# A two-layer encoder on one core: prepared weight sums paused, respaced and extended to the second mixer, and one affine step moved to ScalarE

## The chip, the cores and the metric

The kernel runs on one core of a Trainium2 chip. The core has TensorE (PE in the profile, with PEld for its weight loads), VectorE (DVE), ScalarE (ACT), GpSimd (POOL) and SyncE (SP, which here only issues transfers). The metric is device time in microseconds, the median of several runs; before the change it is 2389.23 us (2387.51 to 2389.99 in three runs). The shape is a batch of 1, a sequence of 256 tokens, a model width of 2048, all in float32.

## What is computed

```python
def reference(x, ...):
    h = x
    for layer in range(2):
        hn = rmsnorm(h, norm_mix_g[layer])
        if layer == 0:
            mix = mlstm_mixer(hn, ...)   # 8 heads, matrix memory, both directions, head norm, gate, @ w_out
        else:
            mix = hgrn_mixer(hn, ...)    # 16 heads, gated linear recurrence, both directions, head norm, gate, @ w_out
        h = h + mix
        h = h + conv_glu(rmsnorm(h, norm_ffn_g[layer]), ...)   # (gelu(conv3(a)) * v) @ w_down, width 5504
    return rmsnorm(h, final_g)

def gate(f):                             # inside hgrn_mixer
    log_f = jnp.logaddexp(log(lb), log1p(-lb) + jax.nn.log_sigmoid(f))   # f -> lb + (1 - lb) * sigmoid(f)
    k = (1.0 - lb) * jax.nn.sigmoid(-f)
```

So there are six stages, one after the other: the first mixer, its output projection, the first feed-forward part, the second mixer, its output projection, the second feed-forward part. Each feed-forward part again has two halves (`FA` = 22 and `FB` = 21 blocks of 128 columns), each an up-projection followed by a down-projection.

## The kernel before

**Products and splits.** Every product with a weight is made from two halves of each operand: a value is copied to the PE's reduced float32 type (`wh`, on ACT, L145), and the rest is the difference (`wl`, on DVE, L146). `split_weights` does this in pieces of 1024 columns, in the order in which the products need them, and PE uses three of the four products of halves. A raw weight tile (`raw`, 2048 columns, 1 MB, three buffers) is loaded by SP and holds two pieces. The halves of a piece have four buffers each (`WB`), in some stages two more.

**Chunks.** `stream` walks through a list of chunks. A chunk of kind `fm` makes a 256-wide projection with features on partitions (L342, L346), a chunk of kind `tm` a 512-wide one with tokens on partitions (L358). A chunk of kind `st` (`squares_by_seven`, L232) makes two 512-wide column blocks of a projection at once: its weights come as units, four blocks B11, B22, B21, B12 of 512 columns each. For the units listed in `SEVEN` and `SEVEN_MIX` it uses seven block products in place of eight. For these it needs differences of the weight blocks and, of the activations, the sums that `token_sums` makes.

**Combines and couples.** The differences of the weight blocks are made in one of two ways. Either `combine` (L204) makes them in place, just ahead of the unit's splits: four differences of 128x512 on DVE. Or they are made ahead, in a stage that has time for them, by `prepare`: SP loads the unit into a pair of tiles (`praw`, two loads of 512 KB), DVE makes four differences (L607), SP stores them to a scratch in HBM (`tscr`, two stores of 512 KB), and the down-projection later loads 768 KB of the unit from the weights, 256 KB from the scratch into the same raw tile, and 768 KB from the scratch into a tile `T`. One unit handled in this way is called a couple here. Couples are counted from 1, within the program or, where it is said, within a stage.

There are two sorts. The couples of a feed-forward half are made during its own up-projection (`ahead` is true: the next couple's load is issued before this couple's differences, with two pairs of tiles). The early couples are made in the mixer ahead of the feed-forward part (`prepare_early`, `ahead` is false): one pair of tiles, so a load has to wait until the store before it has landed. The first mixer makes 12 early couples, the second 15. The pairs of the two output projections (`SEVEN_MIX`, three units each) are combined in place.

**Side work and order.** Everything beside the main stream of products is a generator that is pushed to `side`. `tick` advances a planned time with the matmuls that are emitted (0.65 us for a few, 20.8 us for a `tm` chunk and 10.4 us for an `fm` chunk), and a job goes on when its own `yield` time is over. This sets the order in which instructions are emitted. A scheduler then orders them again, engine by engine, by when it expects their inputs; a few are pinned. `late` issues a transfer on SP and keeps it in program order against the other ones issued so. Each engine then runs its instructions in that order, and an instruction that waits holds all those behind it.

**The heads.** In the first mixer `head` makes the scores S of one head (L798), multiplies the weights W with them (L800, DVE), splits the result into `Wh` and `Wl` (L803, ACT; L804, DVE), then makes four products `pn` (L812), each followed by a denominator `rd` (L815, L816) and the scaled output `y` (L818, L820). `finish` norms, gates (L835) and transposes it (L840) and splits it (L365). Two heads run at a time, and the weights W of a later pair are made beside them (L787). In the second mixer `take` makes q and the gates: sigmoid (L982), the other sigmoid (L983), the affine step lb + (1 - lb) * s (L984, DVE), a product on POOL (L985). `head` then multiplies QK by the gates level by level (L1033, DVE; a gathered copy on ACT at L1012; G2 on POOL), makes `pa` and `pd` on PE (L1020, L1044, L1045), merges them into `AD` (L1055, DVE) and `AT` (L1059, ACT), and makes `py` (L1070). `finish` gates and transposes the result (L1085, L1091).

In `mixed`, which makes an output projection, `token` prepares the activation sums (L639, L542). Its temporaries `f` and the combines' tiles `T` share one tag with two buffers.

Of the kernel before, what the change touches and what calls it, by code (L numbers as in the profile page):

```python
# [8 lines left out]
F32 = mybir.dt.float32  # L9
# [6 lines left out]
P = 128  # L16
# [47 lines left out]
def trunk_kernel(ctx, tc, xT, x_d, fg_d, pp_d, cst_d, w_gate, w_first, w_aq, w_ak, w_av, w_ao, w_aout, w_ao2,  # L64
# [22 lines left out]
    def aux(name):  # L87
        return psa.tile([P, 512], F32, tag="aux", name=name)
# [39 lines left out]
    pin = tc.keep_in_program_order  # L128
    turns = dict(w=0)

# [50 lines left out]
    def temporary(pool_, name):  # L181
        return pool_.tile([P, 1536], F32, tag="avc", bufs=TEMP if pool_.name == "ff" else 2, name=name)

# [404 lines left out]
    def prepare(tiles, todo, first, period, finished, start, ahead):  # L588

        loaded = []  # L590

        def load(i):
            if i < len(todo):
                r = tiles(i)
                for j in range(2):
                    start(r[j], todo[i][0][:, j * 1024:(j + 1) * 1024])
                loaded.append(r)

        yield first
        load(0)  # L600
        for i, (_, dst) in enumerate(todo):
            yield period / 2
            if ahead:
                load(i + 1)
            B11, B22, B21, B12 = (loaded[i][j // 2][:, j % 2 * 512:(j % 2 + 1) * 512] for j in range(4))
            for x, y, out in ((B12, B22, B22), (B12, B11, B12), (B11, B22, B11), (B21, B11, B21)):
                dve.tensor_tensor(out, x, y, ALU.subtract)  # L607
                yield period / 24
            for j in range(2):
                nc.sync.dma_start(dst[:, j * 1024:(j + 1) * 1024], loaded[i][j])  # L610
            if not ahead:
                yield period / 3
                load(i + 1)
        finished.append(True)
# [7 lines left out]

    def mixed(w, w2, x, norm, close):

# [6 lines left out]

        two = pair(w2, KT, 1, x, sums, norm, SEVEN_MIX)

        def token():
# [20 lines left out]
    def mlstm(norm, nxt):  # L655
# [135 lines left out]
        def head(st, j):  # L791
            mp, emn = box["mp"], box["emn"]
            hd = 2 * st["pr"] + j
            q, k, V, W = st["q"][j], st["k"][j], st["V"], st["W"][j]
            S = aux("S")
# [27 lines left out]
            for t in range(2):  # L823
                jk = ev.tile([P, 512], F32, tag="jk", bufs=1, name="jk")
                act.activation(jk[:, 0:T], y[:, t], AF.Square, accum_out=ss[:, t:t + 1])
            st["y"][j] = (y, head_scale(ss, 256))

        def finish(st):
            for j in range(2):
                while st["y"][j] is None:  # L830
                    yield
                y, rs = st["y"][j]
                pz = aux("pz")
                for t in range(2):
                    dve.scalar_tensor_tensor(y[:, t], y[:, t], rs[:, t:t + 1], st["sg"][:, t, j * T:(j + 1) * T],  # L835
                                             ALU.mult, ALU.mult)
                yield
                for t in range(2):
                    for v in range(2):
                        pe.transpose(pz[:, v * T + t * P:v * T + (t + 1) * P], y[:, t, v * P:(v + 1) * P], ident)  # L840
                for v in range(2):
                    i = 2 * (2 * st["pr"] + j) + v
                    YT[i] = slot(i, "ya")
                    split(YT[i], pz[:, v * T:(v + 1) * T], col("a_head_g", i))
                yield

        chunks = []
        for pr in range(AH // 2):
# [36 lines left out]
            def done_first(ps, done_v=done_v):  # L885
# [10 lines left out]
                side.push(start(gs))  # L896
                prepare_early(box["mp"], 0, 45.0, 13.0)

# [34 lines left out]
    def hgrn(norm, nxt):  # L933
# [32 lines left out]
        def take(hd, what, ps):  # L966
# [16 lines left out]
            act.activation(kz, z, AF.Sigmoid, scale=-1.0)  # L983
            dve.tensor_scalar(g, g, oml[:, hd:hd + 1], lb[:, hd:hd + 1], ALU.mult, ALU.add)  # L984
            pool.tensor_tensor(QZ[:, (1 - dr) * T:(2 - dr) * T], st["q"], g, ALU.mult)  # L985
# [147 lines left out]

        return chunks + mixed(w_bout, w_bo2, yx, nxt, stack.close)


    def ffn(layer, norm, nxt):
        stack = ExitStack()
        ending = isinstance(nxt, FinalNorm)
        box = dict(n=2 * (len(SEVEN[0]) + len(SEVEN[1])) * layer)  # L1140
        chunks, pairs = [], []
# [36 lines left out]
        for part, (f0, nf) in enumerate(((0, FA), (FA, FB))):  # L1178
# [13 lines left out]
            def two(src, c0, norm, seven, first=0, todo=todo, finished=finished, GT=GT, SX=SX, nf=nf):  # L1192
                ch = pair(src, nf, c0, lambda k: GT[k], lambda u: SX[u], norm, seven)
                ch.waits = [finished]
                for i, u in enumerate(seven):
                    ch.stored[u] = tscr[box["n"]]
                    (early[layer][0] if i < first else todo).append((src[:, 2048 * u:2048 * (u + 1)], tscr[box["n"]]))
                    box["n"] += 1
                if first:
# [117 lines left out]
def build(nc, ins, out_shape=(2, P, D), **kw):  # L1317
# [3 lines left out]
    mscr = nc.dram_tensor("mscr", (64, T), F32, kind="Internal").ap()  # L1321
    tscr = nc.dram_tensor("tscr", (4 * len(SEVEN[0]) + 4 * len(SEVEN[1]), P, 2048), F32, kind="Internal").ap()
    with tile.TileContext(nc, schedule_with_timeline_sim=True) as tc:
# [17 lines left out]
```

## Time and profile before

| | |
|---|---|
| median of the runs | 2389.23 us |
| the profiled execution | 2391.24 us |
| its span, first to last instruction | 2388.9 us |
| granted TensorE clock, mean | 0.998 |
| ScalarE casts `wh` from raw tiles of 1024 columns (L145), 844 of them, with others of the line | 875.1 us |
| VectorE splits `wl` of the same (L146), 844 | 1031.7 us |
| couples' differences (L607), 240 | 167.2 us |

The time of an execution is a little longer than the span of its instructions. Times in the profile are microseconds from the start of the span, means of one instruction are nanoseconds. In the tables by stage a row holds the stretch, its length, the busy time of PE, PEld, DVE, ACT and POOL with the number of instructions in brackets, the granted TensorE clock, the share of time in which the DMA engines were busy, and GB/s. In a table of waits a row reads: who waited, for whom, how long in total, how often, the longest. In a timeline a row begins with the start and the time taken; at its end, in brackets, stands how long the engine was idle before it and what ended that. In a table of groups the idle time before the instructions stands behind the second bar. In the chain of waits a row is a start, a time and what took it. A row of transfers ends with the size of one and the median time from issue to landing.

### The profile page before, as it was taken

To read this page: it belongs to the slowest core of one execution; us is meant where nothing else is said; L and a number is where in the kernel's file an instruction comes from. 1 tells how busy PE (TensorE), PEld (TensorE's weight loads), DVE (VectorE), ACT (ScalarE), POOL (GpSimd) and SP (SyncE) were. 2 spreads that over 40 slices of the span, in tenths; PEclk is the share of its full clock that TensorE was granted. 3 is DMA by queue.
4 is the path that set the end of the run, shared out by engine and by line. 5 is a ranking of instruction groups with operands and counts; after the bars stand their busy time and mean duration, and the time that the engine had idled before them with its cause. 6 is when DMAs were issued, how large, how long until landed. Compare 5 with 4: busy or idle time off the path is not lost.

```text
span 2388.9 us, 38320 instructions
## 1 busy us (share of the span) xinstructions
PE 2367.0 (99%) x14548; PEld 2019.7 (85%) x14548; DVE 1972.0 (83%) x3060; ACT 1442.5 (60%) x2289; POOL 217.3 (9%) x244
## 2 busy tenths in 40 slices
PE   9999999999999999999999999999999999999998
PEld 8878888888888888888888888887888888888886
DVE  7777787897888888787898888878788788888787
ACT  7655555555665555665666666665555566555565
POOL 0100000000000000000243333220000000000000
PEclk9999999999999999999999999999999999999999
DMA  8778756886698887786766777545788588887695
GB/s 306 266 263 294 279 194 212 300 302 231 227 346 288 324 307 248 279 308 222 246 235 253 248 247 248 207 167 180 254 298 289 194 303 315 287 286 252 207 343 199
DMA packets 119240, 624.31 MB, mean 261 GB/s; under 512 B 13440, under 2 KB 13952, under 8 KB 74256
## 3 DMA queue, kind: packets, MB, share of 16 engines
q1 hardware_dynamic: 117360, 617.86, 73.3%
q0 software_dynamic: 1120, 3.21, 0.7%
q8 instruction: 114, 1.87, 0.3%
q10 hardware_dynamic: 576, 0.79, 0.1%
q14 instruction: 70, 0.57, 0.1%
HBM read 556.73 MB, written 65.08 MB: 260 GB/s over the span
## 4 chain that ended last, share of the span: by engine, by line
PE 85%; DMA 7%; DVE 5%; issue 2%; ACT 1%; POOL 0%; SPq 0%; DVEq 0%; POOLq 0%; ACTq 0%
PE mm L342 32%; PE mm L346 16%; PE mm L358 14%; PE pc L232 13%; PE mm L232 7%; DMA praw<-in_w_d 4%; DVE wl L146 2%; DMA tscr<-praw 1%; DVE praw L607 1%; PE py L1070 1%; PE pd L1020 0%; PE pz L419 0%; PE pa L1020 0%; ACT wh L145 0%; DMA T<-tscr 0%
## 5 line engine op out<-in xcount | busy, mean ns | idle before, releaser
L342 PE MATMUL mm<-xt,wh 128*128 128x512 f32 x3776 | 1313.5, 394 | 0.1
L146 DVE TENSOR_TENSOR wl<-raw,wh 128x1024 fp32r<-128x1024 f32 (+1 forms) x844 | 1031.7, 1228 | 217.0 <-ACT wh L145 213.3
L145 ACT CAST wh<-raw 128x1024 fp32r<-128x1024 f32 (+1 forms) x844 | 875.1, 1042 | 486.4 <-PE mm L342 280.6
L346 PE MATMUL mm<-xt,wl 128*128 128x256 f32 x3776 | 1044.5, 278 | 0.3 <-DVE wl L146 0.3
L342 PEld LDWEIGHTS mm<-xt,wh 128*128 128x128 f32 x3776 | 705.7, 188 | 160.5 <-issue 0.2
L346 PEld LDWEIGHTS mm<-xt,wl 128*128 128x128 f32 x3776 | 709.7, 188 | 6.2 <-DVE wl L146 0.9
L358 PE MATMUL mm<-wh,xt 128*128 128x512 f32 x1024 | 323.6, 394 | 0.2 <-ACT wh L145 0.2
L232 PE MATMUL pc<-wh,g 128*128 128x512 f32 x776 | 260.9, 390 | 0.2 <-ACT wh L145 0.2
L607 DVE TENSOR_TENSOR praw<-praw 128x512 f32<-128x512 f32 x240 | 167.2, 697 | 80.6 <-DMA praw<-in_w_d 63.7
L358 PEld LDWEIGHTS mm<-wh,xt 128*128 128x128 f32 x1024 | 191.4, 188 | 40.1 <-ACT xt L364 0.6
L358 PE MATMUL mm<-wl,xt 128*128 128x512 f32 x512 | 198.6, 392 | 0.0
L232 PEld LDWEIGHTS pc<-wh,g 128*128 128x128 f32 x776 | 145.6, 188 | 30.9 <-ACT wh L145 0.6
L232 PE MATMUL pc<-wl,g 128*128 128x512 f32 x388 | 150.9, 389 | 0.0
L232 PE MATMUL mm<-wh,sx 128*128 128x512 f32 x396 | 140.2, 390 | 0.5 <-ACT wh L145 0.4
L146 DVE TENSOR_TENSOR wl<-T,wh 128x512 fp32r<-128x512 f32 (+1 forms) x132 | 124.0, 953 | 20.1 <-ACT wh L145 19.6
L145 ACT CAST wh<-T 128x512 fp32r<-128x512 f32 (+1 forms) x132 | 109.6, 835 | 38.7 <-PE pc L232 14.1
L566 POOL TENSOR_TENSOR hm<-hm,u 128x512 f32<-128x512 f32 x10 | 14.7, 1467 | 1230.1 <-DVE u L565 637.5
L1033 DVE TENSOR_TENSOR QK<-QK,G 128x256 f32<-128x256 f32 x224 | 110.0, 537 | 8.3 <-ACT kq L1012 8.1
L1012 ACT COPY kq<-QK 128x512 f32<-128x512 f32 x112 | 74.6, 669 | 68.5 <-DVE QK L1033 46.6
L358 PEld LDWEIGHTS mm<-wl,xt 128*128 128x128 f32 x512 | 96.5, 188 | 18.9
L1157 ACT COPY avc<-mm 128x256 f32<-128x256 f32 x172 | 64.1, 373 | 77.3 <-PE mm L346 77.1
L232 PEld LDWEIGHTS mm<-wh,sx 128*128 128x128 f32 x396 | 74.2, 188 | 16.6 <-ACT wh L145 1.3
(237 smaller groups left out, 2240.3 us busy)
## 6 DMA issues: line engine op xcount, KB each, us to landing
raw<-in_w_up SPq DMA_DIRECT2D x172, 1024.0 KB, 5.3
praw<-in_w_d SPq DMA_DIRECT2D x120, 512.0 KB, 7.0
tscr<-praw SPq DMA_DIRECT2D x120, 512.0 KB, 6.4
raw<-in_w_bq SPq DMA_DIRECT2D x48, 1024.0 KB, 5.0
raw<-in_w_d SPq DMA_DIRECT2D x60, 768.0 KB, 6.0
T<-tscr SPq DMA_DIRECT2D x60, 768.0 KB, 7.1
raw<-in_w_ao SPq DMA_DIRECT2D x24, 1024.0 KB, 5.3
raw<-in_w_d SPq DMA_DIRECT2D x24, 1024.0 KB, 6.7
```

What stands on the lines that cost most here:

```text
L145: pin(act.copy(wh[:, :m], r))
L146: pin(dve.tensor_tensor(wl[:, :m], r, wh[:, :m].bitcast(F32), ALU.subtract))
L232: pe.matmul(ps, a, b, start=id(ps) not in begun, stop=stop and i == 2)
L342: pe.matmul(ps[f], wh[:, c:c + P], x, start=k + kk == 0, stop=False)
L346: pe.matmul(ps[f][:, 0:T], wl[:, c:c + P], x[:, 0:T], start=False, stop=k + kk == ch.nk - 1)
L358: pe.matmul(ps[t], x[:, a + t * P:a + (t + 1) * P], w[:, c], start=st and i == 0, stop=sp and i == 2)
L566: pool.tensor_tensor(part(1, 0), part(1, 0), u, ALU.add)
L607: dve.tensor_tensor(out, x, y, ALU.subtract)
L1012: act.copy(m, blocks(QK, h))
L1033: dve.tensor_tensor(two[:, j], two[:, j], by[:, j], ALU.mult)
L1070: pe.matmul(py[:, c], AT[:, s if s == t else 2 + s], V[:, s, j * P:(j + 1) * P], start=(s == 0), stop=(s == 1))
L1157: act.copy(z, p[:, T:2 * T])
```

## The change

- `turns["busy"]` counts the first mixer's heads that are at work: `head` raises it at its start and lowers it at its end, `finish` does so for each of its two heads. An unfinished couple emits no further difference while the count is above 0.
- In `prepare`, the early couples wait a period less 6 us between load and differences (in place of half a period), 0.6 us between differences, and 3 us between the store and the next load (in place of a third of a period). The waiting third of a period now stands in the branch for the couples of a feed-forward half, which had none at this place. The first mixer's early couples start at 40 in place of 45 with a period of 12 in place of 13, the second's have a period of 18 in place of 20.
- The three units of the second output projection become early couples of the second mixer, ahead of the 15 that it makes. The pair waits until all early couples are done.
- Temporaries outside the feed-forward parts get a tag by their name, with two buffers each.
- The affine step of the second mixer's gate goes from DVE to ACT.

```diff
-    turns = dict(w=0)
+    turns = dict(w=0, t=0, busy=0)
...
     def temporary(pool_, name):
-        return pool_.tile([P, 1536], F32, tag="avc", bufs=TEMP if pool_.name == "ff" else 2, name=name)
+        ff = pool_.name == "ff"
+        return pool_.tile([P, 1536], F32, tag="avc" if ff else name, bufs=TEMP if ff else 2, name=name)
...
         for i, (_, dst) in enumerate(todo):
-            yield period / 2
             if ahead:
+                yield period / 2
                 load(i + 1)
+            else:
+                yield period - 6.0
             B11, B22, B21, B12 = (loaded[i][j // 2][:, j % 2 * 512:(j % 2 + 1) * 512] for j in range(4))
             for x, y, out in ((B12, B22, B22), (B12, B11, B12), (B11, B22, B11), (B21, B11, B21)):
+                while turns["busy"]:
+                    yield 0.6
                 dve.tensor_tensor(out, x, y, ALU.subtract)
-                yield period / 24
+                yield period / 24 if ahead else 0.6
             for j in range(2):
                 nc.sync.dma_start(dst[:, j * 1024:(j + 1) * 1024], loaded[i][j])
-            if not ahead:
+            if ahead:
                 yield period / 3
+            else:
+                yield 3.0
                 load(i + 1)
...
+    def store(ch, src, u, todo):
+        ch.stored[u] = tscr[turns["t"]]
+        turns["t"] += 1
+        todo.append((src[:, 2048 * u:2048 * (u + 1)], ch.stored[u]))
...
-    def mixed(w, w2, x, norm, close):
+    def mixed(w, w2, x, norm, close, layer=None):
...
+        if layer is not None:
+            for u in SEVEN_MIX:
+                store(two, w2, u, early[layer][0])
+            two.waits = [early[layer][1]]
...
         def head(st, j):
...
+            turns["busy"] += 1
...
             st["y"][j] = (y, head_scale(ss, 256))
+            turns["busy"] -= 1
...
-                prepare_early(box["mp"], 0, 45.0, 13.0)
+                prepare_early(box["mp"], 0, 40.0, 12.0)
...
-            prepare_early(mp, 1, 30.0, 20.0)
+            prepare_early(mp, 1, 30.0, 18.0)
...
-            dve.tensor_scalar(g, g, oml[:, hd:hd + 1], lb[:, hd:hd + 1], ALU.mult, ALU.add)
+            act.activation(g, g, AF.Identity, bias=lb[:, hd:hd + 1], scale=oml[:, hd:hd + 1])
...
-        return chunks + mixed(w_bout, w_bo2, yx, nxt, stack.close)
+        return chunks + mixed(w_bout, w_bo2, yx, nxt, stack.close, 1)
```

More of the change, by code (lines that the diff above doesn't have):

```diff
@@ L832, in finish @@
                 y, rs = st["y"][j]
+                turns["busy"] += 1
                 pz = aux("pz")
@@ L844, in finish @@
                     split(YT[i], pz[:, v * T:(v + 1) * T], col("a_head_g", i))
+                turns["busy"] -= 1
                 yield
@@ L1139, in ffn @@
         ending = isinstance(nxt, FinalNorm)
-        box = dict(n=2 * (len(SEVEN[0]) + len(SEVEN[1])) * layer)
+        box = {}
         chunks, pairs = [], []
@@ L1195, in two @@
                 for i, u in enumerate(seven):
-                    ch.stored[u] = tscr[box["n"]]
-                    (early[layer][0] if i < first else todo).append((src[:, 2048 * u:2048 * (u + 1)], tscr[box["n"]]))
-                    box["n"] += 1
+                    store(ch, src, u, early[layer][0] if i < first else todo)
                 if first:
@@ L1321, in build @@
     mscr = nc.dram_tensor("mscr", (64, T), F32, kind="Internal").ap()
-    tscr = nc.dram_tensor("tscr", (4 * len(SEVEN[0]) + 4 * len(SEVEN[1]), P, 2048), F32, kind="Internal").ap()
+    tscr = nc.dram_tensor("tscr", (len(SEVEN_MIX) + 4 * len(SEVEN[0]) + 4 * len(SEVEN[1]), P, 2048), F32, kind="Internal").ap()
     with tile.TileContext(nc, schedule_with_timeline_sim=True) as tc:
```

## The prediction

> **What bounds the kernel.** I read the page's busy shares, then busy time by stage, then PE's waits in each stage, then the lines of DVE just ahead of those waits.
>
> ```profile
> span 2388.9 us, 38320 instructions
> PE 2367.0 (99%) x14548; PEld 2019.7 (85%) x14548; DVE 1972.0 (83%) x3060; ACT 1442.5 (60%) x2289; POOL 217.3 (9%) x244
> ...
> 60.00:331.00 271.00, 266.38 (x1352) 223.30 (x1352) 203.12 (x377) 147.20 (x243) 19.24 (x25) 1.00 0.77 268
> 331.00:394.00 63.00, 63.00 (x292) 52.27 (x291) 57.25 (x81) 38.87 (x57) 3.56 (x2) 1.00 0.55 191
> 394.00:1093.00 699.00, 698.68 (x3736) 599.99 (x3735) 585.36 (x839) 413.31 (x596) 16.43 (x9) 1.00 0.80 284
> 1093.00:1613.00 520.00, 517.58 (x4684) 444.64 (x4683) 439.03 (x758) 349.85 (x666) 155.30 (x177) 1.00 0.66 230
> 1613.00:1683.00 70.00, 67.17 (x303) 53.78 (x302) 60.73 (x89) 39.05 (x59) 3.54 (x2) 1.00 0.50 176
> 1683.00:2378.00 695.00, 694.70 (x3717) 596.77 (x3716) 576.23 (x827) 407.11 (x585) 15.49 (x13) 1.00 0.77 272
> ```
>
> The stages are, in order, the first mixer, its output projection, the first feed-forward part, the second mixer, its output projection, the second feed-forward part. In each row the length comes first and PE's busy time second. PE is the bound throughout; what can be won is its idle time: 4.6, 0, 0.3, 2.4, 2.8 and 0.3 us. Idle time of DVE or ACT is worth nothing by itself. PE's waits in the first, fourth and fifth of these stages:
>
> ```profile
> PE pz L840 <- DVE y L835: 1.6, 2, 0.9
> PE pn L812 <- DVE Wl L804: 1.4, 2, 1.1
> PE pn L812 <- DVE y L820: 0.7, 1, 0.7
> PE pn L812 <- ACT Wh L803: 0.6, 1, 0.6
> ...
> PE py L1070 <- ACT AT L1059: 2.1, 1, 2.1
> ...
> PE pc L232 <- ACT wh L145: 1.4, 2, 1.0
> PE pc L232 <- DVE wl L146: 1.0, 1, 1.0
> PE mm L232 <- ACT wh L145: 0.4, 1, 0.4
> ```
>
> In the mixers' heads they have one cause. DVE works in order and stands at a couple's first difference (L607) until its load lands; the head's own DVE work is queued behind it:
>
> ```profile
> 166.43 0.69 DVE L607 TENSOR_TENSOR praw<-praw 128x512 f32<-128x512 f32 x1 [3.71 <-DMA praw<-in_w_d]
> ...
> 295.62 0.69 DVE L607 TENSOR_TENSOR praw<-praw 128x512 f32<-128x512 f32 x1 [3.62 <-DMA praw<-in_w_d]
> ...
> 145.45 0.62 PE L358 MATMUL mm<-wh,xt 128*128 128x512 f32 x2
> ...
> 295.72 0.40 PE L358 MATMUL mm<-wl,xt 128*128 128x512 f32 x1
> 297.24 0.51 PE L812 MATMUL pn<-Vh,Wl 128*128 128x258 f32 x2 [1.13 <-DVE Wl L804]
> ...
> 1259.86 0.69 DVE L607 TENSOR_TENSOR praw<-praw 128x512 f32<-128x512 f32 x1 [3.55 <-DMA praw<-in_w_d]
> ...
> 1262.91 1.16 PE L1070 MATMUL py<-V,AT 128*128 128x128 f32 x8 [2.10 <-ACT AT L1059]
> ```
>
> A late load (3.62) makes the split Wl late, and PE stands for 1.13. A stall costs somewhat more than its idle time, because matmuls overlap: two take 0.62, one 0.40, so they start 0.22 apart, and idle counts only from the end of the last one, 0.18 later. I add 0.2 per stall. The ceiling is then 4.3 + 6 x 0.2 = 5.5 us in the first mixer and 2.8 + 4 x 0.2 = 3.6 us in the second output projection. In the second mixer the stall brought a second loss:
>
> ```profile
> 1260.50:1262.90 2.40, 0.31 (x2) 0.00 (x0) 2.40 (x8) 0.99 (x5) 0.00 (x0) 1.00 0.03 14
> ...
> 1264.25:1267.65 3.40, 3.40 (x10) 2.62 (x9) 3.40 (x7) 2.47 (x5) 0.00 (x0) 0.50 0.73 251
> ```
>
> After a stretch with 0.31 us of PE work in 2.40, the granted clock was 0.50 for 3.40 us, which is 1.7 us of work lost. This event cost 2.1 + 0.2 + 1.7 = 4.0 us. [...] All that can be won is 5.5 + 4.0 + 3.6 + 0.6 = 13.7 us.
>
> **The change part by part.** *The pause.* A couple's differences are no longer emitted between the steps of a first-mixer head. In the built order of the kernel before, those of couples 1, 4, 5, 8, 9 and 12 stand among head operations; in the changed order, where the scheduler still hoists what it thinks ready, those of couples 1, 2, 5 and 9 do. The second halves of the heads and the finishing (L835) are nearly free of them. Couples 5 and 9 now stand between the next head's W and the first rd, where couple 1 stood before; the row of that place is the 0.7 of L820, so 0.9 each. Of 5.5 us I take 5.5 - 1.8 = 3.7 as gained. Bounds: 5.5 if nothing stalls, 0 if the hoisted couples cost what the old ones did.
>
> *The couples' cycle.* This is the part that may cost. These rows give the turn of one pair of buffers, and what DVE waited for it in the first and in the second mixer:
>
> ```profile
> 107.78 7.01 DMA tscr<-praw
> ...
> 114.80 5.93 DMA praw<-in_w_d
> ...
> praw<-in_w_d SPq DMA_DIRECT2D x120, 512.0 KB, 7.0
> tscr<-praw SPq DMA_DIRECT2D x120, 512.0 KB, 6.4
> ...
> T<-tscr SPq DMA_DIRECT2D x60, 768.0 KB, 7.1
> ...
> L607 DVE TENSOR_TENSOR praw<-praw 128x512 f32<-128x512 f32 x48 | 33.0, 687 | 36.9 <-DMA praw<-in_w_d 28.3 <-issue 8.5
> ...
> L607 DVE TENSOR_TENSOR praw<-praw 128x512 f32<-128x512 f32 x60 | 43.8, 730 | 11.2 <-DMA praw<-in_w_d 10.4 <-issue 0.7
> ```
>
> Store, then load, then differences: 6.4 + 7.0 = 13.4 us from a couple's last difference to the next one's first, if the load is issued when the store lands. Early couples used to pause a third of the period before a load (4.3 planned us in the first mixer, 6.7 in the second); now it is 3.0 in both. The second mixer takes 520 us for 416 planned (8 chunks of 20.8, 24 of 10.4), a factor of 1.25: 8.3 us of pause was over 6.4, 3.75 is not. So SP will stand at each load for up to 6.4 - 3.75 = 2.7 us, with the weights' raw loads queued behind it and ACT's casts waiting for those; three raw buffers of two pieces each cover it. The longer lead (12 planned us for 10) does not decide, since the scheduler sets a difference on DVE where it expects the load. What decides is the DVE work between couples. These rows price it:
>
> ```profile
> L146 DVE TENSOR_TENSOR wl<-raw,wh 128x1024 fp32r<-128x1024 f32 x167 | 208.9, 1253 | 39.0 <-ACT wh L145 38.1
> L1033 DVE TENSOR_TENSOR QK<-QK,G 128x256 f32<-128x256 f32 x224 | 110.0, 537 | 8.3 <-ACT kq L1012 8.1
> ...
> L1055 DVE COPY_PREDICATED AD<-cst,pd 128x64 f32<-128x64 int32 x80 | 18.1, 227 | 7.3 <-ACT AD L1053 6.0
> L984 DVE TENSOR_SCALAR G<-G,oml,lb 128x256 f32<-128x256 f32 x32 | 15.9, 498 | 0.5 <-ACT G L982 0.5
> ```
>
> In the second mixer of the kernel before, every gap between couples holds six to ten splits; in the changed order nine of seventeen gaps hold two to five. The gap before the fourth couple holds 4 splits, 8 QK products and 4 AD copies: 4 x 1.25 + 8 x 0.54 + 4 x 0.23 = 10.2 us, 3.2 short of 13.4. Nine such waits are some 29 us of DVE standing, for 11.2 now. In the first mixer twelve couples (36.9 us of such waits) mostly passed PE by: splits run ahead, and only what falls on a head's chain reaches PE. Of the nine, the fourth couple has four AD copies of a nearly finished head close behind it, the place of the 3.55 above; the others stand among QK products or evacuations. I take one event of 4.0 us, as before: no gain, no loss. Bounds: 4.0 gained if none; three events, 8 us lost.
>
> [...]
>
> In the feed-forward parts the swapped branch adds a third of a period to each cycle, so couples spread over the whole part. PE stands there for 0.3 + 0.3 us; I take 0.4 of it, between 0.6 and a loss of 1.
>
> *Second mixer's pair made ahead.* It removes three units' combines from the output projection:
>
> ```profile
> L204 DVE TENSOR_TENSOR T<-raw 128x512 f32<-128x512 f32 x6 | 4.0, 686 | 2.9 <-PE pz L1091 2.9
> ...
> L204 DVE TENSOR_TENSOR T<-raw,T 128x512 f32<-128x512 f32 x3 | 2.0, 686 | 0.0
> L204 DVE TENSOR_TENSOR raw<-raw 128x512 f32<-128x512 f32 x3 | 2.0, 684 | 0.0
> ```
>
> That is 12 differences, 4.0 + 2.0 + 2.0 = 8.0 us of DVE, in a stage in which DVE is busy for 60.7 of 70. PE's stalls there wait for splits, and for casts of differences, that are queued behind them, so I take 3.0 of the 3.6. The first output projection keeps its combines and has no idle at all, so such a stage can run clean; that is the upper bound, 3.6. What comes in: per unit two loads and two stores of 512 KB, and for all three 12 x 0.69 = 8.3 us of DVE, in the second mixer, where DVE is free for 520 - 439 = 81 us; and in the projection a T load (7.1 us) and a quarter of the raw tile from scratch, per unit. They are issued while SP runs ahead; if a T buffer (there are two) came free late, SP would hold raw loads back and nothing would be won: lower bound 0. The couples must be done before the pair starts: 30 + 18 x (17.4 + about 0.8 of rounding to steps) = 358 planned us, of 416.
>
> *The affine step.* 32 operations leave DVE (15.9 us) and go to ACT. The nearest row on ACT, the same function on the same shape with two column operands:
>
> ```profile
> L1162 ACT ACTIVATE avc<-avc,pp 128x256 f32<-128x256 f32 x43 | 25.8, 600 | 26.0 <-DVE avc L1160 25.9
> ```
>
> So 32 x 0.60 = 19.2 us on ACT, which is free for 520 - 350 = 170. The built order has as many table loads as before. Queued behind it are the second sigmoid and the weight casts, each later by 0.6 at most; POOL's product starts about as early. On the path: 0, within half a microsecond either way.
>
> The other edits (own tags for two temporaries, more scratch) issue nothing new. Sum: 3.7 + 0 + 0.4 + 3.0 + 0 = 7.1 us. The profiled execution took 2391.24, 2.0 over the median of the runs, 2389.23: 2391.2 - 7.1 = 2384.1 there, and 2389.2 - 7.1 = 2382.1 as a median.
>
> **Rivals.** First, *the second mixer gives it back*: two events instead of one, 4.0 more, 2386.1. For it: nine short gaps. Against: the other 11.2 - 3.55 = 7.6 us of such waits leave no mark on PE there now. Second, *the heads are no better*: four couples still stand in them, the first mixer gains nothing, 2385.8. Against: the gaps before couples 5 and 9 hold a whole head's DVE work, so their loads should have landed. Third, *slower*: DVE, once late, stays late in the second mixer, because it is 84% busy (439 of 520) and makes up only 1 us in 6. From three more events on (12.0 more), the time is 2382.1 + 12.0 = 2394.1. It decides once a wait of 3 us reaches PE at four of the nine gaps. Fourth, *better*: no event at all, 2378.1.
>
> **How the numbers follow.** Forecast 0.48, rivals 0.17, 0.13, 0.10 and 0.12. A measurement of this kernel tells about 0.2% (4.8 us) from no change, so faster is under 2384.4: forecast and fourth rival, 0.60; same is the first two rivals, 0.30; slower 0.10. The likeliest case spans 2378 to 2384.4; the range, 2376.5 to 2391.5, reaches from just under the ceiling of 13.7 across both same cases and a part of the way to the third rival.
>
> **What would show it.** Right: no PE wait at L840's place and at most two short ones at L812's; no combine rows and no PE wait at L232's in the second output projection; PE's clock at 0.5 at most once in the second mixer; waits of L607's there of 20 to 35 us. Wrong: PE waits of several us at L1044's, L1070's or L1091's in the second mixer, or differences still named ahead of late Wl and y.

## The result, and the profile after

The changed kernel takes 2395.9 us (median of 8 runs, 2393.9 to 2399.1); the kernel before took 2388.4 beside it (8 runs, 2386.0 to 2391.2). The ratio is 1.0031, with a 95% interval of 1.0020 to 1.0042. The change made the kernel slower by 7.5 us; 7.1 us faster had been forecast, and the time lies above the range. Stage times and rows are of one profiled execution each: here one of 2399.13 us, the slowest of the eight, with this span and these stages (first the page, then busy time by stage, the rows of both mixers and of the second output projection):

```profile
span 2397.1 us, 38319 instructions
...
PE 2368.0 (99%) x14548; PEld 2022.4 (84%) x14548; DVE 1959.6 (82%) x3028; ACT 1458.8 (61%) x2321; POOL 204.2 (9%) x244
```

```profile
60.00:331.00 271.00, 265.55 (x1350) 223.94 (x1349) 207.69 (x392) 150.85 (x247) 16.94 (x25) 0.99 0.78 268
...
394.00:1093.00 699.00, 699.00 (x3746) 601.18 (x3745) 586.10 (x840) 415.18 (x597) 16.45 (x9) 1.00 0.81 284
1093.00:1613.00 520.00, 509.07 (x4626) 435.95 (x4625) 423.46 (x725) 357.00 (x684) 143.76 (x176) 0.99 0.69 239
1613.00:1683.00 70.00, 69.64 (x321) 57.28 (x320) 55.29 (x83) 42.15 (x68) 4.24 (x3) 1.00 0.62 217
```

DVE has less to do and ACT a little more, as the edit of the affine step says; neither is the bound. In the second mixer PE's idle time went from 2.4 to 10.9 us; in the second output projection it went from 2.8 to 0.4. Measured from the first matmul of a stage to that of the next, so that stages of shifted kernels can be compared, in us:

```
                   first mixer  projection  feed-forward  second mixer  projection  feed-forward   span
before                   280.1        88.8         696.3         495.3        97.1         693.2  2388.9
after                    280.7        88.7         694.0         507.5        93.4         693.2  2397.1
```

The second mixer lost 12.2 us and its projection won 3.7. The 2.3 us of the first feed-forward part aren't the change's: two kernels below whose instructions up to the second mixer stand in the order of the kernel before (e7 and e8) took 696.6 and 694.0 there, and their first mixers 279.2 and 278.7, for 280.1; the first mixer of e12, in the same order again, took 277.2. So up to 2.9 us of a stage can come from the execution alone, and a smaller difference between two profiles says something only where the medians of the runs say it too.

PE's waits in the second mixer now (who waits, for whom, in total, how often, the longest), where the kernel before had one row of 2.1:

```profile
PE pa L1064 <- DVE QK L1053: 4.2, 2, 3.1
PE mm L359 <- DVE wl L146: 2.3, 1, 2.3
PE pz L1111 <- DVE y L1105: 1.8, 2, 1.6
PE py L1090 <- ACT V L1123: 1.2, 1, 1.2
PE pd L1040 <- issue: 0.7, 2, 0.5
PE pd L1040 <- DVE yb L366: 0.7, 1, 0.7
```

The timeline of the same stage shows where they come from. Lines have moved by some 20: the couples' differences are L612 now. In brackets stands how long the engine stood before the instruction.

```profile
1249.72 0.69 DVE L612 TENSOR_TENSOR praw<-praw 128x512 f32<-128x512 f32 x1 [3.82 <-issue]
...
1253.87 0.50 PE L359 MATMUL mm<-wl,xt 128*128 128x512 f32 x1 [2.29 <-DVE wl L146]
...
1329.32 1.42 DVE L612 TENSOR_TENSOR praw<-praw 128x512 f32<-128x512 f32 x2 [4.56 <-issue]
...
1332.69 0.46 PE L1064 MATMUL pa<-QK 128*128 128x128 f32 x2 [3.05 <-DVE QK L1053]
...
1409.96 0.69 DVE L612 TENSOR_TENSOR praw<-praw 128x512 f32<-128x512 f32 x1 [4.65 <-issue]
...
1410.88 1.01 ACT L1079 COPY AT<-AD 32x64 f32<-32x64 f32 x4 [4.10 <-DVE AD L1075]
...
1413.17 0.49 PE L1090 MATMUL py<-V,AT 128*128 128x128 f32 x2 [1.18 <-ACT V L1123]
...
1498.16 0.69 DVE L612 TENSOR_TENSOR praw<-praw 128x512 f32<-128x512 f32 x1 [5.53 <-DMA praw<-in_w_d]
...
1505.58 0.30 PE L1111 MATMUL pz<-cst,y 128*128 128x128 f32 x1 [1.57 <-DVE y L1105]
```

Four times DVE stood for more than 3 us at a couple's first difference, and each time PE was held up a little later, by what was queued behind that difference on DVE: a split, a QK product, a copy into AD, a gated y. The third goes by way of ACT: it stood 4.10 us for the AD copy just behind the difference, and the V that PE waited for was queued behind ACT's AT copies. Two of the four had the half clock behind them, as the one event of before had; the rows below, busy time in short stretches, show each idle stretch and the slow one after it (the clock is the third figure from the end):

```profile
1251.60:1253.90 2.30, 0.03 (x1) 0.03 (x1) 2.30 (x5) 2.30 (x3) 0.96 (x1) 1.00 0.00 0
...
1255.60:1259.00 3.40, 3.40 (x133) 3.02 (x132) 3.40 (x5) 2.15 (x7) 0.00 (x0) 0.50 0.81 271
...
1329.63:1332.69 3.06, 0.01 (x2) 0.03 (x1) 3.03 (x6) 0.27 (x1) 0.00 (x0) 1.00 0.23 96
...
1334.50:1337.70 3.20, 3.20 (x46) 2.66 (x36) 3.20 (x8) 1.02 (x4) 0.00 (x0) 0.52 0.94 342
```

So 8.5 us more of idle time and one slow stretch more (1.7 us) give 10.2 of the 12.2 us; the other 2.0 were not traced (eight more stalls at the prediction's 0.2 us each would be 1.6).

Why the couples' data come late is seen on SP (its own timeline; the second figure is the time from a group's first issue to the end of its last):

```profile
1234.36 1.26 SPq L615 DMA_DIRECT2D tscr<-praw  x2
1242.98 1.55 SPq L381 DMA_DIRECT2D praw<-in_w_d  x2
...
1486.89 0.33 SPq L615 DMA_DIRECT2D tscr<-praw  x1
1487.27 6.58 SPq L381 DMA_DIRECT2D praw<-in_w_d  x2
```

Behind a couple's store (L615) the next load is the next thing in SP's queue, so SP stands until the store has landed: from 1235.6 to 1243.0, and between the two halves of the load at 1487.27. SP's waits for this and DVE's waits at the differences (busy time, mean ns, idle time before; first differences and the others together) in the second mixer:

```profile
SPq L381 <- DMA tscr<-praw: 27.9, 12, 7.3
```

```profile
L612 DVE TENSOR_TENSOR praw<-praw 128x512 f32<-128x512 f32 x72 | 51.4, 714 | 28.5 <-issue 15.1 <-DMA praw<-in_w_d 13.1
```

The kernel before has no SP row of this kind in that stage, and 11.2 us at the differences. The load of the third of the four waits was late for another reason: three raw loads were ahead of it on SP, the last store lay 17 us back.

In the first mixer an event of the same kind is new. The second couple stands between the steps of a pair's heads, and y (L854), 8 us later, is late for the transpose:

```profile
103.68 0.69 DVE L612 TENSOR_TENSOR praw<-praw 128x512 f32<-128x512 f32 x1 [5.89 <-DMA praw<-in_w_d]
...
111.54 0.88 DVE L854 SCALAR_TENSOR_TENSOR y<-y,rs,sg 128x256 f32<-128x256 f32 x2 [0.84 <-POOL rs L517]
...
112.17 1.08 PE L859 MATMUL pz<-cst,y 128*128 128x128 f32 x4 [3.14 <-DVE y L854]
```

In the second output projection one short wait is left:

```profile
PE pc L233 <- DVE wl L146: 0.4, 1, 0.4
```

### The profile page after: what moved, and what is told of

The parts are those of the page before. It is cut to its first block, busy times and chain, and to the rows that moved or that the text cites. A ratio compares the mean times of both kernels' runs of the same rounds, so it can differ in the third digit from the quotient of the medians.

```text
span 2397.1 us, 38319 instructions
## 1 busy us (share of the span) xinstructions
PE 2368.0 (99%) x14548; PEld 2022.4 (84%) x14548; DVE 1959.6 (82%) x3028; ACT 1458.8 (61%) x2321; POOL 204.2 (9%) x244
## 4 chain that ended last, share of the span: by engine, by line
PE 88%; DMA 5%; DVE 4%; issue 2%; ACT 1%; POOL 1%; SPq 0%; DVEq 0%; POOLq 0%; ACTq 0%
PE mm L343 34%; PE mm L347 17%; PE pc L233 13%; PE mm L359 13%; PE mm L233 8%; DMA praw<-in_w_d 3%; DMA tscr<-praw 2%; DVE wl L146 1%; DVE QK L1053 1%; DVE praw L612 1%; PE pn L829 1%; PE pz L420 0%; PE py L1090 0%; PE pd L1040 0%; POOL QK L1005 0%
## 5 line engine op out<-in xcount | busy, mean ns | idle before, releaser
L612 DVE TENSOR_TENSOR praw<-praw 128x512 f32<-128x512 f32 x252 | 174.9, 694 | 54.5 <-DMA praw<-in_w_d 37.1
```

## Experiments

All runs were made beside runs of the kernel before (medians 2388.2, 2388.6, 2387.6 and 2387.9 us in the four groups: 1 to 4, 5 to 8, 9 to 11, 12). "Rest" is the planned pause between a couple's store and the next load, "lead" that between load and differences. In the first four expectations the second mixer is counted up to the projection's first seven-product unit; so counted it took 520.3 us before and 532.6 after, in the table's way 495.3 and 507.5. All stage times in us, by the same measure as above:

```
                  second mixer  2nd projection  first mixer  couples over 3 us late in 2nd mixer   ratio [95%]
before                   495.3            97.1        280.1   1
after                    507.5            93.4        280.7   4      1.0031 [1.0020, 1.0042]
e1_affine_dve            499.7            93.4        279.3   1      1.0008 [0.9999, 1.0018]
e2_rest7                 495.6            93.4        280.0   1      0.9991 [0.9982, 1.0001]
e3_no_pair               500.9            94.6        279.4   4      1.0015 [1.0006, 1.0025]
e4_no_pause              506.5            93.4        285.5   5      1.0057 [1.0041, 1.0073]
e5_rest_both             495.9            93.4        279.8   1      0.9988 [0.9978, 0.9998]
e6_rest7_dve             500.2            93.4        280.3   4      1.0011 [1.0001, 1.0020]
e7_before_affine         491.6            97.1        279.2   1      0.9983 [0.9972, 0.9993]
e8_before_rest3          498.2            97.1        278.7   2      1.0017 [1.0008, 1.0027]
e9_no_pair_rest7         493.8            94.6        279.5   1      0.9987 [0.9977, 0.9996]
e10_period20             497.1            93.4        279.7   2      0.9993 [0.9984, 1.0003]
e11_two_sets             498.8            96.2        279.2   2      1.0024 [1.0013, 1.0034]
e12_affine_tags          491.3            94.6        277.2   0      0.9972 [0.9960, 0.9983]
```

**Which edit costs, from the changed kernel.** Each of the first four undoes one part of the change.

e1_affine_dve, the affine step back on DVE:

```diff
-            act.activation(g, g, AF.Identity, bias=lb[:, hd:hd + 1], scale=oml[:, hd:hd + 1])
+            dve.tensor_scalar(g, g, oml[:, hd:hd + 1], lb[:, hd:hd + 1], ALU.mult, ALU.add)
```

> The changed kernel with the affine step back on DVE alone. In the changed kernel's profile the second mixer takes 532.6 us from its first to the next stage's first matmul, 520.3 before. Theory A (the couples' cycle: the load now follows its store by 3 planned us, so it waits for the store, and DVE waits for the load at gaps of few splits): the second mixer stays at 529 to 535 us, differences wait 22 to 35 us there, ratio to before 1.002 to 1.004. Rival B (the affine step on ACT delays the gates): the second mixer falls to 520 to 524 us, ratio 0.998 to 1.000.

2390.2 us. The second mixer wins back 7.8 of the 12.2 us; counted as in the expectation it takes 524.7, under theory A's range and just over rival B's. DVE's waits at the differences are halved, while SP still stands for the stores 12 times:

```profile
L612 DVE TENSOR_TENSOR praw<-praw 128x512 f32<-128x512 f32 x72 | 51.4, 714 | 14.5 <-issue 11.1 <-DMA praw<-in_w_d 3.2
```

```profile
SPq L381 <- DMA tscr<-praw: 20.1, 12, 5.5
```

So SP's standing for the stores alone doesn't make the loss: with the step on ACT four couples are late by over 3 us, with it on DVE one. That DVE, with 15.9 us of work less, reaches the late loads earlier and so stands longer is a likely reason, not a shown one, and e6 below speaks against it as a rule.

e2_rest7, in the second mixer a rest of 7 for 3, taken from the lead:

```diff
-                yield period - 6.0
+                yield period - 3.0 - rest
...
-                yield 3.0
+                yield rest
...
-            prepare_early(mp, 1, 30.0, 18.0)
+            prepare_early(mp, 1, 30.0, 18.0, 7.0)
```

> The changed kernel with, in the second mixer alone, 7 planned us between a couple's store and the next load and 8 between load and differences, in place of 3 and 12; the period, 18, and the 18 couples stay. Theory A: the store has landed before the load's turn, differences wait at most 15 us in all there (28 in the changed kernel), the second mixer takes 520 to 525 us, ratio to before 0.997 to 1.000. Rival C (three more couples in the stage are what costs) and rival B: no change, 529 to 535 us, ratio 1.002 to 1.004.

2385.8 us, and the second mixer is at 495.6, with the affine step on ACT, all 18 couples and a shorter lead. Counted as in the expectation it takes 520.6, as theory A had it; DVE's waits, 16.1, are a little over its 15. PE has no single wait over 1.0 there. One load is late by over 3 us here too (4.34 at 1490.80); the wait that it leaves on PE, for y at 1495.30, is 0.97. SP's waits for the stores have all but gone, and DVE's waits have shrunk:

```profile
SPq L381 <- DMA tscr<-praw: 6.1, 4, 2.5
```

```profile
L612 DVE TENSOR_TENSOR praw<-praw 128x512 f32<-128x512 f32 x72 | 51.8, 719 | 16.1 <-DMA praw<-in_w_d 12.4 <-issue 3.2
```

e3_no_pair, without the three units of the second output projection as couples:

```diff
-        return chunks + mixed(w_bout, w_bo2, yx, nxt, stack.close, 1)
+        return chunks + mixed(w_bout, w_bo2, yx, nxt, stack.close)
```

> The changed kernel without the second output projection's three couples (combined in place again, as before); 15 couples with the new cycle and the period of 18. Theory A: thirteen of the gaps between couples are as short as in the changed kernel, so the second mixer still takes 526 to 532 us, and the output projection is back at about 72 us (68.4 in the changed kernel); ratio 1.001 to 1.004. Rival C: the second mixer takes 520 to 523 us, ratio 0.998 to 1.000.

2392.1 us. The second mixer is 6.6 us shorter without them (525.9 as the expectation counts, just under theory A's range), with four late couples as in the changed kernel. Its projection is only 1.2 us longer, 94.6, and not back at 97.1, as had been expected; so most of what the projection won has nothing to do with the couples.

e4_no_pause, without the pause while a first-mixer head works:

```diff
-                while turns["busy"]:
-                    yield 0.6
```

> The changed kernel without the pause for heads at work; the new cycle stays. In the profiles the first mixer from its second chunk to the output projection takes 280.7 us in the changed kernel and 280.1 before. If the pause is worth what was forecast (3.7 us) and something else took it away, this takes 283 to 287 us. If the pause only moves the waits from one place of the heads to another, 279 to 283 us. Second mixer within 2 us of 532.6, since its emission is the same.

2402.3 us: the first mixer takes 285.5, 4.8 more. The pause does what it says; but the first mixer with it is no shorter than the one before, which had no pause and a rest of 4.3. The new cycle costs there about what the pause wins.

**Whether the rest is the cause, and what the affine step does alone.** e5_rest_both has a longer rest in the first mixer as well:

```diff
-                prepare_early(box["mp"], 0, 40.0, 12.0)
+                prepare_early(box["mp"], 0, 40.0, 12.0, 6.0)
```

> Like e2_rest7, and in the first mixer too the rest from a couple's store to the next load is longer: 6.0 planned us for 3.0, out of the lead (period still 12.0). Theory A (the short rest issues the load late against where the scheduler set its differences, in both mixers): the waits of the first mixer's couples shrink from some 37 us to under 25, its three stalls of 3.1, 1.4 and 0.9 us shrink to under 2.5 together, the first mixer goes from 280.0 us to 276 to 278, and the time is 2 to 4 us under that of e2_rest7. Rival B (in the first mixer it is the place of the hoisted couples among a head's operations that counts, not the rest): the first mixer stays within 1 us of 280 and so does the time.

2384.2 us; the first mixer stays at 279.8, as rival B had it. The waits of its couples were 21.2 us in the changed kernel (the 37 of the expectation are of the kernel before) and are 27.3 here, so the longer rest doesn't even shorten them.

e6_rest7_dve is e2_rest7 with the affine step back on DVE (the diff of e1).

> Like e2_rest7, with the affine step back on DVE. Theory A (the affine step on ACT cost much in the changed kernel only because it moved DVE's order against loads that came late; with a long rest it is worth nothing by itself): second mixer within 1.5 us of e2_rest7's 495.6, time within 2 us. Rival C (the affine step on ACT lengthens the gate's own chain, whatever the couples do): second mixer 3 us or more shorter than in e2_rest7, time too.

2391.2 us: neither held. The second mixer is 4.6 us *longer* with the step on DVE. Four couples are late by over 3 us here, for one in e2, though SP stands for stores for only 4.6 us and other transfers lie between store and load before each of the four; so loads can come late without the short rest. PE waits for AT, which is at the end of a head's DVE chain:

```profile
PE py L1090 <- ACT AT L1079: 4.8, 4, 2.4
```

Rest and affine step can't be priced apart. With the step on ACT the rest of 7 in place of 3 takes the second mixer from 507.5 to 495.6 us and the time from 2395.9 to 2385.8. With the step on DVE it changes next to nothing: 499.7 and 500.2, 2390.2 and 2391.2 (e1 and e6).

e7_before_affine is the kernel before with the affine step on ACT as its one edit (the diff of e1 turned round).

> The kernel before with the affine step on ACT as its only edit. Theory A: second mixer within 2 us of the 495.3 of the kernel before, and the time within 2 us. Rival C: second mixer longer by 4 to 8 us (what the same step brought in the changed kernel: 507.5 with it, 499.7 without), time 2392 to 2397.

2384.0 us, faster than before, with an interval of the ratio of 0.9972 to 0.9993; again neither held. The second mixer is 3.7 us shorter: the one event of before, 2.10 at AT with the half clock behind it, has shrunk to 1.0 and has no slow stretch:

```profile
PE py L1070 <- ACT AT L1059: 1.0, 1, 1.0
```

So the same step wins 3.7 and 4.6 us in two kernels and costs 7.8 in a third. Where it costs, it brings three more couples that are late by over 3 us (e1 to after), where it wins 4.6, three fewer (e6 to e2), and where it wins 3.7, the one stays one. It moves DVE's order, and with it which loads come late; no run held that order fixed, so this is a reading and not shown.

e8_before_rest3 is the kernel before with the short rest in the second mixer alone, all else as before:

```diff
-            yield period / 2
+            yield period / 2 if rest is None else period * 5 / 6 - rest
...
-                yield period / 3
+                yield period / 3 if rest is None else rest
...
-                          todo, first, period, finished, late, False))
+                          todo, first, period, finished, late, False, None if layer == 0 else 3.0))
```

> The kernel before with one edit: in the second mixer the rest from a couple's store to the next load is 3.0 planned us for 6.7, given to the lead, with the period still 20.0 and still 15 couples. Theory A (the short rest is enough): waits of the couples' first differences there go from 11.2 us to 20 or more, PE stalls of over 1 us at three places or more, second mixer 3 to 10 us longer than 495.3. Rival D (the short rest costs only together with three more couples and the shorter period, which leave DVE no room): second mixer within 2 us of 495.3.

2391.6 us (3.0 more than the kernel before beside it), second mixer 2.9 us longer, 15.5 us of waits at the differences: between the two. By itself, with the step on DVE, the short rest costs only a quarter of the 12.2. But SP's waits for the stores are there at once, though the period is 20 and there are 15 couples:

```profile
SPq L380 <- DMA tscr<-praw: 17.4, 11, 5.1
```

**What the pair made ahead costs, and whether it is the wait of the load.** e9_no_pair_rest7 is e2_rest7 without the pair (the diff of e3) and with a period of 20.

> The changed kernel without the couples of the second output projection, and in the second mixer a rest of 7.0 planned us for 3.0 and a period of 20.0 for 18.0; the affine step stays on ACT, the pause, the spread and the temporaries' own tags stay. Theory A (in the second mixer only the affine step helps, when loads come in time, and the pair's three couples cost more there than the projection wins): second mixer 491 to 493 us as in e7_before_affine, second output projection 94.6 as in e3_no_pair, time 2380 to 2383, under that of e2_rest7 by 2 to 4. Rival E (the pair costs nothing when the rest is long): second mixer near the 495.6 of e2_rest7, time within 1.5 us of e2_rest7.

2384.6 us, 1.2 under e2_rest7 as rival E had it; the second mixer, 493.8, lies between the two. e10_period20 is the same with the pair:

```diff
-            prepare_early(mp, 1, 30.0, 18.0, 7.0)
+            prepare_early(mp, 1, 30.0, 20.0, 7.0)
```

> Like e2_rest7 with all its 18 couples, but a period of 20.0 planned us for 18.0, the room given to the lead. Theory A1 (the three couples cost 4 to 5 us in the second mixer because the period is tighter): second mixer 491 to 493.5, second output projection 93.4, time 2379 to 2382. Rival A2 (they cost by their mere number, each 4 operations of 0.7 us and 2 MB of transfers more): second mixer 494.5 to 497, time within 1.5 us of e2_rest7.

2386.2 us. The two differ by the pair alone: in their profiles it costs 3.3 us in the second mixer (493.8 to 497.1) and wins 1.2 in the projection. The medians differ by 1.6 us, and the intervals of the two ratios overlap, so the loss is small and its size uncertain. The room in the period brings nothing (497.1 is at the end of A2's range); whether couples cost by their number or by where they fall was not told apart.

e11_two_sets leaves the rest at 3 and gives the couples two sets of tiles, so that a load has no store to wait for:

```diff
-MIX = 5
+MIX = 4
...
-        side.push(prepare(lambda i: [mp.tile([P, 1024], F32, tag=f"p{j}", name="praw") for j in range(2)],
+        side.push(prepare(lambda i: [mp.tile([P, 1024], F32, tag=f"p{j}", bufs=1 + layer, name="praw") for j in range(2)],
...
-            y = mp.tile([P, T], F32, tag="y", bufs=4, name="y")
+            y = mp.tile([P, T], F32, tag="y", bufs=3, name="y")
```

> The changed kernel with two sets of praw tiles in the second mixer, so that a couple's load needs no longer wait for the store before it; rest 3.0 and period 18.0 stay. To make room one of five kq buffers and one of four y buffers are left out. Theory A (what costs is the wait of the load for the store): SP's waits at the loads go, the couples' waits fall from 28.5 us to under 12, second mixer 494 to 498 us for 507.5. Rival F (what costs is where the short rest puts the differences in DVE's order, not the late data): second mixer over 503 us. By either theory the buffers left out may cost 1 to 2 us.

2392.2 us. SP has no row of waits for the stores any more, and the second mixer takes 498.8: 8.7 of the 12.2 us are gone, with the short rest in place. DVE's waits are at 20.6 us, more than was expected, two loads are late by over 3 us with no store to wait for, and the projection lost 2.8 us; the two buffers left out are part of this run, and how much they cost wasn't tried alone. It goes against rival F, as far as that.

**A version from what was left.** e12_affine_tags is the kernel before with two edits, the affine step on ACT and the temporaries' own tags.

> The kernel before with two edits alone: the affine step on ACT, and the temporaries' own tags. Theory A (the affine step is worth 3.7 us where loads come in time, and the 2.5 us by which e3_no_pair has a shorter second output projection than the kernel before come from the tags): second mixer 491 to 493, second output projection 94.6, time 2380.5 to 2383.5, ratio about 0.997 to 0.998. Rival G (the shorter projection came from where the second mixer left off, not from the tags): projection 97, time about 2384.

2381.2 us (7 runs, 2378.5 to 2384.2), a ratio of 0.9972 with an interval of 0.9960 to 0.9983: it beats both kernels. The second mixer takes 491.3, the projection 94.6. Theory A holds throughout. Against e7, which lacks only the tags, the projection goes from 97.1 to 94.6: the tags, which issue nothing new but let `f` and `T` have two buffers each, win 2.5 us. No couple of the second mixer is late by 3 us any more. From 1093 to 1626 us PE has two waits left (the first is in the projection), and from 1093 to 1613 it is busy for 519.1 of 520:

```profile
PE pc L233 <- DVE wl L146: 1.4, 1, 1.4
PE py L1071 <- ACT AT L1060: 0.9, 1, 0.9
```

```profile
1093.00:1613.00 520.00, 519.14 (x4702) 446.44 (x4701) 431.08 (x731) 363.40 (x693) 137.98 (x177) 1.00 0.66 230
```

## Why the prediction was wrong

**The step that failed** is in the part on the couples' cycle: "I take one event of 4.0 us, as before: no gain, no loss." It had found the cause, a rest shorter than the store's landing, had nine short gaps, and put DVE's standing at some 29 us; 28.5 were measured. It then let one of the nine reach PE, on the ground that only couples beside AD copies of a nearly finished head matter and that those among QK products or evacuations don't. The runs show the other: all four waits over 3 us reached PE, through a split, a QK product, an AD copy and y, for 2.29, 3.05, 1.18 and 1.57 us. They are those of the 7th, 10th, 13th and 17th couple of the stage; the fourth, which the prediction had named, waited 0.61. The second mixer lost 12.2 us. Undoing the rest (e2) takes 11.9 of it back, and taking away the store that the load waits for (e11) 8.7, so the turn of the one pair of buffers is the cause, together with the affine step: without that (e1) 7.8 is back too, with the rest as it was. This is the third rival as written, down to its point ("a wait of 3 us reaches PE at four of the nine gaps") and its price of 12.0; it had been given a chance of 0.10. That its sum fits so closely is partly luck: it put 4.0 us on each event, half clock included, where two of the four had none, it took all the waits to be the short rest's, where the third was not, and it counted a gain in the first mixer that didn't come. What spoke for it stood in the prediction too: DVE makes up only 1 us in 6. It was outweighed by the first mixer, where most of twelve such waits passed PE by.

**SP** was to stand "up to 2.7 us at each load". It stood 2.3 on average but up to 7.3, because in the built order a load can follow its store at once; the planned pause is not what the queue keeps. The sum took the landings from the rows of the kernel before, 6.4 us for a store and 7.0 for a load; in the changed kernel the medians are 6.4 and 6.4.

**The affine step**, priced at 0, was the second error, in both directions: 3.7 us won alone in the kernel before (e7), 4.6 with the long rest (e2 against e6), 7.8 lost in the changed kernel (e1). ACT's time was priced right (0.60 us each; measured 0.59, 19.0 us in all). The price left out what the move does to DVE: the wait at AT, the one event of before, goes from 2.1 to 1.0 (e7), and from 4.8 to 0.6 between e6 and e2. Why the same step costs with the short rest stays open. DVE stands 14.0 us longer there (28.5 for 14.5), because it comes to the late loads earlier or because its order changes; with the long rest the step shortens DVE's waits instead (21.7 to 16.1, e6 to e2).

**The pause** was to win 3.7 us and won nothing on the whole (280.1 before, and 277.2 to 279.2 in e7, e8 and e12, whose first mixers are in the order of before; 279.2 to 280.7 in the kernels that have it). It is worth 4.8 us in the changed cycle (e4), and that cycle, with couple 2's new event in it (3.14 us, and the clock at 0.50 for 3.4 us behind it), costs about as much. The prediction priced couples 5 and 9, which now wait for nothing, and left couple 2 at nothing, which waits for 5.89. A longer rest didn't help there (e5). So the second rival was right about the sum, for a partly other reason.

**The pair made ahead** won 3.7 in its projection for 3.0, but 2.5 of that came from the tags that were written off as issuing nothing (e3, e9, e12); the couples give 1.2. Their 8.3 us of DVE work, covered on paper by 81 us of free time, cost 6.6 us of PE time with the short rest (e3) and some 3 with the long one (e10 against e9, one profile each). A sum of free time over a stage says nothing about where the work falls.

**The feed-forward parts**: 0.4 us can't be seen; the difference of 2.3 comes and goes in kernels that are alike there.

The sum: the forecast stood 13.8 us under the result. The second mixer makes 12.2, the pause 3.7 and the feed-forward parts 0.4, the projection gives 0.7 back: 15.6, and the 1.8 over are within what single executions differ by.

## What to carry to other kernels

Where one pair of buffers turns through load, work and store, look at the *built* queue: if the next load stands right behind the store, the issuing engine can stand for the landing (here SP, up to 7.3 us, 27.9 in the stage) and the engine that works after it (here DVE, 28.5 us), and the longer lead in the plan, 12 us for 10, didn't help here. When such waits are counted on an engine that feeds the bound through several short chains, count each long one as reaching the bound unless its place shows otherwise: here DVE was busy for 423.5 of 520 us, and all four waits of over 3 us reached PE, for 1.18 to 3.05 us each. Try the parts of a change one by one: here two edits alone make 2381.2 us, all of them together 2395.9, and the part taken for a neutral one changed its sign with another part. Undoing one part shows what that part is worth beside the others, not what it is worth alone.

## What the runs showed of the hardware

The first 20 us and the end left out, the granted clock fell to 0.50 once in the profiled execution of the kernel before, at 1264.25, and three times in that of the changed kernel, at 112.17, 1255.63 and 1334.14. Each time it stayed there for 3.4 us:

```profile
112.17:115.57 3.40, 3.40 (x12) 2.97 (x13) 2.82 (x5) 3.40 (x7) 1.59 (x1) 0.50 0.55 141
...
1255.63:1259.03 3.40, 3.40 (x133) 3.05 (x132) 3.40 (x4) 2.12 (x7) 0.00 (x0) 0.50 0.82 275
...
1334.14:1337.55 3.41, 3.41 (x74) 2.87 (x61) 3.41 (x8) 1.33 (x5) 0.28 (x1) 0.50 0.94 338
```

PE's idle stretch ahead was 2.10 us long in the kernel before and 3.14, 2.29 and 3.05 us in the changed one. PE had begun again at 1262.91, 112.17, 1253.87 and 1332.69, so the clock fell up to 1.8 us after that (at 1255.63 after 1253.87).

The length of the idle stretch doesn't decide by itself. In e4 the clock was 0.50 behind a wait of 2.0 us (first row). In e6 it was 1.00 over the whole 100 us in which a wait of 2.4 lies (second row), and in e11 it was 1.00 behind one of 2.6 (the last two):

```profile
1509.60:1511.50 1.90, 1.90 (x8) 1.61 (x7) 1.66 (x4) 1.45 (x4) 1.81 (x3) 0.50 0.96 384
...
1400.00:1500.00 100.00, 94.74 (x886) 81.56 (x884) 82.45 (x149) 62.47 (x128) 23.59 (x26) 1.00 0.71 255
...
1191.60:1193.00 1.40, 1.40 (x9) 1.21 (x9) 0.00 (x0) 0.57 (x1) 0.00 (x0) 1.00 0.98 415
1193.00:1196.00 3.00, 3.00 (x19) 2.64 (x18) 1.23 (x1) 2.11 (x6) 0.00 (x0) 1.00 0.09 33
```

What tells the two sorts apart was not shown here.
